# A decoder trunk in fp32r products: twelve norms summed by two fp32r products with ones, and the engines' order planned anew with a table of moved groups

## The chip, the cores and the metric

The kernel runs on one core of one Trainium2 chip. The metric is the device time of one execution in microseconds (us), the median over runs. The core has five engines with an instruction stream each: TensorE (PE; its weight loads are PEld in the profile), VectorE (DVE), ScalarE (ACT), GpSimd (POOL) and SyncE (SP, which here only issues DMAs). They wait for each other through semaphores, and each of them takes its instructions strictly in the order in which they stand in its stream.

## The reference

Two layers of a decoder trunk over one sequence of 1024 tokens with 1024 channels, in float32:

```
for l in range(DEPTH):
    h = rmsnorm(x, attn_norm[l]);  proj = h @ w_in[l]
    y_a = mla_attention(...)        # 4 heads, latent q and kv with norms of their own, rope, causal
    y_b = short_gated_conv(...)     # width 3
    y_c = multiscale_pool(...)      # trailing means over 2, 4, 8, 16
    y_d = swa_sink_attention(...)   # window 128, ALiBi, sinks
    mixed = rmsnorm of each of the four groups (256 channels each) * mix_norm
    x = x + mixed @ w_o[l]
    h2 = rmsnorm(x, ffn_norm[l]);  gate, up = split(h2 @ w_gate_up[l])
    x = x + (silu(gate) * up) @ w_down[l]
return rmsnorm(x, final_norm)
```

rmsnorm(x) is x / sqrt(mean(x*x) + 1e-6) times a gain, over the channels. d_ff is 2816.

## The kernel before

All activations lie with channels on the 128 partitions and tokens along the free dimension; a token half is 512 columns, and a tile of 128 x 512 float32 fills one of the eight PSUM banks. A product of two float32 operands is made of three fp32r products (`mm3`, line 270): each operand is split into a high part (a copy to fp32r on ACT, line 281 or, with a gain, 284) and a low part (the difference, on DVE, line 282 or 285); high*high, high*low and low*high are summed in PSUM. `half_split` does that for one tile of 128 x 512, into two half slots of a pool of 47 pairs of SBUF slots. Weights are loaded by SP and split in the same way (`weights`, lines 213 and 214, and others). The FFN's products are made by a Strassen-like scheme with fewer block products; POOL makes the sums of weights and some of the elementwise products.

A norm needs the sum of squares over all channels. `SumSq.add` (lines 311 to 322) squares a tile on ACT and adds it on DVE to an accumulator of 128 x 512, and `rnorm` sums the accumulator over the partitions with one float32 matmul with a 128 x 128 matrix of ones (line 328), which leaves the sum on all partitions of a bank. In the trace such a float32 matmul stands in two rows. Then ACT takes Ln, Exp and Square (lines 330 to 332) and DVE finishes with a Newton step (333 and 336). The factor is multiplied in after the projection, so the products that follow a norm don't wait for it, only the evacuations of their banks do. There are 35 norms: two at the entry (`enter_norm`), in each layer twelve of groups, latent q and kv and the attention output (`group_scale`, `sq_kv`, `sq_q`, `norm_a`), two of the FFN's input (`norm`), two between the layers, and three at the end, where the last token half goes in two pieces of 256 columns.

The program is written once in a plain order. `order_engines` (line 1914) then decides in what order each engine issues: `steps_of` turns the instructions into steps (neighbouring float32 matmuls onto the same bank are one step) with their dependences and an estimated length, and `arrange` is a list scheduler that plays the five engines against each other in time. A step enters when its inputs are ready and its tiles have a buffer; of the ready steps of an engine that with the lowest rank, its place in the program, is issued. Its prices are tables: 226.7 ns for a product 512 wide, 867 ns for a float32 one with ones, 92 ns for changing over to float32 steps, hand-overs of 25 to 80 ns between engines, DMA landings by size, and others. The result is fixed by extra dependences from each instruction to the one before it on its engine. Buffers of a tag (the PSUM banks: 2 `mm`, 3 `s`, 2 `t`, 1 `pv`) are handed out in the order of the program whatever the ranks are.

In time: 0 to 25 us the entry, to about 400 the first layer's attention part (the projections and short mixers, then from about 200 on the MLA heads with scores at lines 888 to 890, transposes at 942, values at 954 and the pieces of the output projection), to about 1050 its FFN, to about 1420 the second layer's attention part, to 2050 its FFN, and then the last norm and stores.

Of the kernel before, what the change touches and what calls it, by code (L numbers as in the profile page):

```python
# [18 lines left out]
P = 128  # L19
# [92 lines left out]
def trunk_kernel(ctx: ExitStack, tc: tile.TileContext, ins, out):  # L112
# [20 lines left out]
    ident = cst[:, CC_ID : CC_ID + P]  # L133
    ones = cpool.tile([P, P], F32, name="ones")
    dve.memset(ones, 1.0)
    e_r = cpool.tile([P, P], F32R, name="e_r")
    nsink = cpool.tile([P, L * 4], F32, name="nsink")
    nffn = cpool.tile([P, L * NK], F32, name="nffn")
# [157 lines left out]
    class SumSq:  # L296
# [24 lines left out]
            else:  # L321
                dve.tensor_tensor(out=a, in0=a, in1=q, op=ALU.add)

        def rnorm(self, t, cols=whole, tag="t"):

            a, n = F.ap(self.acc[t])[:, cols], self.n
            p = ps(tag)[:, cols]
            pe.matmul(p, ones, a, start=True, stop=True)  # L328
            r0, q = tmp("tn")[:, cols], tmp("tn")[:, cols]
            act.activation(r0, p, AF.Ln, scale=1.0 / n)  # L330
# [30 lines left out]
    def enter_norm(t):  # L361
        for k in range(NK):
            ss.add(t, F.ap(xf[k][t]))
            F.free(xf[k][t])
        ratt[t] = ss.rnorm(t)

    def finish(x, t, cols):

# [10 lines left out]
    for l in range(L):  # L379
# [644 lines left out]
        def norm_a(t):  # L1024
            for c in range(2):
                sg.add(t, F.ap(y["a"][c][t]))
            r = sg.rnorm(t)
            ma = []
            for c in range(2):
                a = F.ap(y["a"][c][t])  # L1030
                mul_to(a, a, F.ap(r))
                ma.append(half_split(a, pcol(l, PC_MIX + c)))
                F.free(y["a"][c][t])
            F.free(r)
            return ma
# [377 lines left out]
                    cur.extend(dn_acts_split(*r))  # L1413

        def norm(u):
            r2.append(F.ap(ss2.rnorm(HALVES[u], tag="pv")))

        std.append(GateUp(2))
        plain(0, 0)
# [162 lines left out]
        for n, (c, m) in enumerate(units):  # L1582
            if n < 5:
                for _ in range(3):
                    next(sums, None)
            if n + 2 < len(units):
                raws.append(dn_raw(*units[n + 2]))
            if c in fresh:
                u, t = fresh[c]
                d = 2 * m + u  # L1590
                x[d][t] = F.half()
                sp.dma_start(F.ap(x[d][t]), xr[d][:, t * HT : (t + 1) * HT])
            if n + 1 < len(units):
# [12 lines left out]
            for j in range(NG):  # L1606
                accumulate(p, w, c, j)
                if m == NM - 1:
                    for s in cur[j]:
                        R.free(s)  # L1610
            for v in w:
                v.free()
            evac(c, m, p)
            for _ in range(2):
                if cn is not None and m < NM - 1:
                    nxt.extend(dn_acts(cn, (len(nxt) + 1) // 2))
            if m == NM - 1:
                cur, nxt = nxt, []
            if c == T3:
                done(2 * m, 0)  # L1620
            elif c == T4:
                done(2 * m + 1, 0)
                done(2 * m + 1, 1)
            elif c == B22:
                done(2 * m, 1)
                if m == 0:
                    expect_layer(l + 1)
                    ahead()
                if m == 1:
                    ratt[0] = ss.rnorm(0, tag="pv")  # L1630
                if m == NM - 1:
                    ratt[1] = ss.rnorm(1, tag="pv")
# [20 lines left out]
    "SP": {"PE": 50, "DVE": 35, "ACT": 35, "POOL": 80, "SP": 30},  # L1653
}
OVERLAP = {"DVE": 82, "ACT": 97, "POOL": 44}
FUNC_SETS = {"Silu": "Silu", "Exp": "Exp", "Ln": "Exp"}
ENGINES = {"PE": "PE", "DVE": "DVE", "Activation": "ACT", "Pool": "POOL", "SP": "SP"}


class Step:  # L1660
    __slots__ = ("ins", "eng", "rank", "before", "after", "tiles", "left", "ns", "tail", "ready", "sums", "bank", "onchip", "size", "start", "end", "table", "ls", "slotafter")

    def __init__(self, eng, rank):
        self.ins, self.eng, self.rank = [], eng, rank
        self.before, self.after, self.tiles = set(), [], set()
# [3 lines left out]
        self.table = None  # L1669


def areas(a):
# [60 lines left out]
def steps_of(tc):  # L1733
    steps, seen = [], {}
    table, runs = None, {"Silu": [], "Exp": []}
    for i in tc.nc.cur_bb.bb.instructions:
# [14 lines left out]
        if eng == "PE":  # L1751
            n = width(outs[0])
            if fp32:
                one = i.ins[1].bass_ap.tensor.name.startswith("ones")
                v.ns += (867 if n == 512 else 534) if one else 108
                v.tail = 163 if one else 122
            else:
                v.ns = MM_NS[n]
                v.tail = 164 if n > 128 else 173
        elif kind == "InstDMACopy":  # L1760
            v.size = 4
            for s, n in outs[0].ap:
                v.size *= int(n)
            if eng == "POOL":
                v.ns, v.tail = 700, 4200
        else:
            v.ns = length(eng, kind, i, ins, outs)
            v.onchip = not any(a.bass_ap.tensor.name.startswith("ps_") for a in ins + outs)
            if eng == "ACT" and len(outs) > 1:
                v.tail = 61  # L1770
        f = FUNC_SETS.get(str(getattr(i, "func", "")).split(".")[-1])
# [8 lines left out]
        for a, writes in [(a, False) for a in ins] + [(a, True) for a in outs]:  # L1780
# [5 lines left out]
            if name.split("_")[0] not in DRAM_TILES:  # L1786
                v.tiles.add(name)
            seen.setdefault(name, [])
            for r, w, u in seen[name]:
                cross = name.startswith("ps_") and not (w or writes)  # L1790
                if cross or (w or writes) and any(
                    x[0] < y[1] and y[0] < x[1] and x[2] < y[3] and y[2] < x[3]
                    for x in r
                    for y in rects
                ):
                    v.before.add(u)
            seen[name].append((rects, writes, v))
    for v in steps:
        v.before.discard(v)
    return steps  # L1800


def arrange(steps, rank=lambda v: v.rank):
# [20 lines left out]
    now = {e: [] for e in SIGNAL}  # L1824
    out = {e: [] for e in SIGNAL}
    wire, pool_busy, last_fp32, table = 0.0, [], False, "Exp"
    for v in steps:
        if not v.left:
            heapq.heappush(later[v.eng], (0.0, rank(v), v.rank, v))
    while any(now.values()) or any(later.values()):  # L1830
        best = None
        for e in SIGNAL:
# [9 lines left out]
        while later[e] and later[e][0][0] <= t:  # L1842
            _, k, n, v = heapq.heappop(later[e])
            heapq.heappush(now[e], (k, n, v))
        k, n, v = heapq.heappop(now[e])
        wait = None
        for name in v.tiles - live:
# [11 lines left out]
        for name in v.tiles - live:  # L1859
            tag = name.rsplit("_", 1)[0]  # L1860
            live.add(name)
            queue[tag].popleft()
# [5 lines left out]
        if v.size:  # L1868
            if e == "SP":
                free[e] = t + 450  # L1870
                wire = max(t + 1400, wire) + v.size / 330.0
                v.end = wire + 600
            else:
                free[e] = t + v.ns
                v.end = t + v.ns + v.tail
# [4 lines left out]
            v.end = s + v.ns + v.tail  # L1880
        else:
            ns = v.ns
            if e == "DVE" and v.onchip:
                ns += 0.8 * sum(max(0.0, min(b, t + ns) - max(a, t)) for a, b in pool_busy[-8:])
            if v.table and v.table != table:
# [6 lines left out]
            if v.tail:  # L1892
                free[e] = v.end - 10
                v.end += v.tail
        out[e].append(v)
        for name in v.tiles:
            todo[name] -= 1
            if not todo[name]:
                tag = name.rsplit("_", 1)[0]
                heapq.heappush(freed[tag], max(u.end for u in uses[name]))  # L1900
                for x in parked[tag]:
                    heapq.heappush(later[x[2].eng], (t + 1, *x))
# [8 lines left out]
    assert sum(map(len, out.values())) == len(steps)  # L1911
    return out

def order_engines(tc):

    info = mybir.DependencyInfo(mybir.DependencyClass.NoSync, mybir.DependencyReason.DATA)
    for queue in arrange(steps_of(tc)).values():
        last = None
        for v in queue:
            for i in v.ins:  # L1920
# [131 lines left out]
```

## Time and profile before

| | |
|---|---|
| median of 3 runs | 2083.02 us (2080.73 to 2083.82) |
| profiled execution | 2081.12 us, span 2079.3 us |
| granted TensorE clock | 0.998 of full |
| PE, DVE, ACT, POOL busy | 2051.7, 1529.5, 968.0, 571.9 us |
| matmuls | 9442 |
| moved by DMA | 289.76 MB, 139 GB/s |

A row of the profile's timeline has the start, the time and the engine, then the line, operation, tile written and tiles read, shapes and how many neighbouring instructions of that kind are merged; in brackets stands the idle time of the engine before it and who ended it. A row of groups has the busy time, the mean duration of one in ns, and the idle time before them. A row of stages (windows) has, for each engine, its busy us and its number of instructions. Matmuls are pipelined: their rows overlap, and a busy PE can still be short of its peak.

### The profile page before, as it was taken

How to read it: one execution, taken by the hardware profiler on the slowest of the kernel's cores; microseconds unless marked ns; L12 is line 12 of the kernel's file. 1: busy time of each engine (PE TensorE's matmuls, PEld its weight loads, DVE VectorE, ACT ScalarE, POOL GpSimd, SP SyncE). 2: the span in 40 equal slices, each digit the busy share in tenths (PEclk: the TensorE clock that was granted, in tenths of full speed). 3: DMA queues.
4: the chain of work that ended last, by engine and by line, in shares of the span. 5: the costliest groups of instructions: out<-in, count | busy, mean ns of one | idle time of the engine just before them, and what ended most of it. 6: DMA issues, size and time to landing. Idle time of an engine off the chain costs nothing.

```text
span 2079.3 us, 26320 instructions
## 1 busy us (share of the span) xinstructions
PE 2051.7 (99%) x9442; PEld 1679.6 (81%) x9442; DVE 1529.5 (74%) x2407; ACT 968.0 (47%) x1700; POOL 571.9 (28%) x453
## 2 busy tenths in 40 slices
PE   8999999999999999999999999999999999999997
PEld 6887777888888888888888877778888888888887
DVE  7878977977776777655657898869777677686555
ACT  6447656643333334444433566656433333354342
POOL 0000000037776775100000000000567677650000
PEclk9999999999999999999999999999999999999999
DMA  4110222424444446966401102232354444398652
GB/s 180 34 51 26 76 83 71 162 80 171 174 155 144 167 162 228 339 233 206 148 27 53 46 16 91 68 118 101 123 185 149 151 167 157 133 323 311 198 177 89
DMA packets 148819, 289.76 MB, mean 139 GB/s; under 512 B 12608, under 2 KB 72000, under 8 KB 148688
## 3 DMA queue, kind: packets, MB, share of 16 engines
q1 hardware_dynamic: 148656, 288.03, 40.1%
q8 instruction: 74, 1.21, 0.2%
q14 instruction: 57, 0.47, 0.1%
q0 software_dynamic: 32, 0.04, 0.0%
HBM read 204.66 MB, written 83.36 MB: 139 GB/s over the span
## 4 chain that ended last, share of the span: by engine, by line
PE 92%; DVE 6%; ACT 1%; DMA 1%; issue 0%; DVEq 0%; ACTq 0%; SPq 0%
PE ps_mm L270 34%; PE ps_s L270 29%; PE ps_t L270 12%; PE ps_pv L270 8%; PE ps_pv L954 2%; PE ps_t L942 1%; DVE u L282 1%; PE ps_s L888 1%; PE ps_pv L564 1%; PE ps_t L328 1%; PE ps_mm L762 1%; PE ps_s L503 1%; PE ps_s L890 1%; PE ps_s L889 1%; DVE u L340 1%; PE ps_t L552 1%
## 5 line engine op out<-in xcount | busy, mean ns | idle before, releaser
L270 PE MATMUL ps_mm<-u,u 128*128 128x512 f32 (+1 forms) x3376 | 825.8, 391 | 9.3 <-ACT u L284 7.1
L270 PEld LDWEIGHTS ps_mm<-u,u 128*128 128x128 f32 x3376 | 617.0, 189 | 131.6 <-ACT u L284 7.1
L270 PE MATMUL ps_s<-u,u 128*128 128x512 f32 x2672 | 630.7, 390 | 0.0
L270 PEld LDWEIGHTS ps_s<-u,u 128*128 128x128 f32 x2672 | 501.6, 188 | 106.3 <-issue 2.2
L282 DVE TENSOR_TENSOR u<-u,u 128x1024 fp32r<-128x1024 f32 (+2 forms) x368 | 443.4, 1230 | 148.7 <-ACT u L281 124.5
L281 ACT CAST u<-u 128x1024 fp32r<-128x1024 f32 (+2 forms) x368 | 321.1, 897 | 476.1 <-PE ps_mm L270 195.8
L270 PE MATMUL ps_t<-u,u 128*128 128x512 f32 (+1 forms) x1212 | 274.4, 379 | 0.0
L270 PEld LDWEIGHTS ps_t<-u,u 128*128 128x128 f32 x1212 | 219.1, 188 | 43.5 <-issue 1.4
L951 POOL MEMSET u<- 128x128 f32 x32 | 6.1, 217 | 865.8 <-PE ps_mm L270 628.8
L159 POOL TENSOR_TENSOR u<-u 128x256 f32<-128x256 f32 x176 | 188.4, 1071 | 68.9 <-DMA u<-in_w_dn 39.8
L1304 POOL TENSOR_TENSOR tp<-tp,u 128x512 f32<-128x512 f32 x88 | 144.0, 1638 | 223.2 <-ACT tp L1303 223.0
L270 PE MATMUL ps_pv<-u,u 128*128 128x512 f32 x696 | 164.9, 389 | 0.0
L270 PEld LDWEIGHTS ps_pv<-u,u 128*128 128x128 f32 x696 | 130.7, 188 | 27.1
L1303 ACT ACTIVATE tp<-tp 128x512 f32<-128x512 f32 x88 | 55.4, 632 | 119.6 <-DVE tp L340 118.6
L1124 POOL TENSOR_TENSOR u<-u,u 128x512 f32<-128x512 f32 x38 | 66.1, 1739 | 144.0 <-DMA u<-in_w_gu 81.9
L284 ACT ACTIVATE u<-u,par 128x512 fp32r<-128x512 f32 x100 | 69.9, 717 | 51.5 <-DVE u L1091 16.9
L282 DVE TENSOR_TENSOR u<-ps_t,u 128x512 fp32r<-128x512 f32 (+4 forms) x136 | 77.5, 584 | 21.7 <-ACT u L281 20.9
L281 ACT CAST u<-ps_t 128x512 fp32r<-128x512 f32 (+4 forms) x136 | 66.7, 505 | 57.0 <-PE ps_t L942 36.0
L285 DVE SCALAR_TENSOR_TENSOR u<-u,par,u 128x512 fp32r<-128x512 f32 x100 | 73.2, 751 | 8.3 <-ACT u L284 8.1
L1516 DVE TENSOR_TENSOR tp<-ps_mm,tn 128x512 f32<-128x512 f32 x38 | 26.3, 692 | 68.7 <-PE ps_mm L270 68.7
L214 DVE TENSOR_TENSOR u<-u,u 128x1024 fp32r<-128x1024 f32 (+1 forms) x46 | 51.8, 1129 | 33.2 <-ACT u L213 12.9
L1146 POOL TENSOR_TENSOR u<-u 128x512 f32<-128x512 f32 x38 | 68.3, 1797 | 8.9 <-DVE u L282 8.9
(186 smaller groups left out, 2240.2 us busy)
## 6 DMA issues: line engine op xcount, KB each, us to landing
u<-in_w_gu SPq DMA_DIRECT2D x88, 512.0 KB, 4.3
ad<-u SPq DMA_DIRECT2D x154, 256.0 KB, 2.5
u<-ad SPq DMA_DIRECT2D x70, 512.0 KB, 5.2
u<-in_w_dn SPq DMA_DIRECT2D x68, 512.0 KB, 3.9
qd<-u SPq DMA_DIRECT2D x44, 512.0 KB, 2.9
u<-qd SPq DMA_DIRECT2D x32, 512.0 KB, 4.7
u<-in_w_in SPq DMA_DIRECT2D x30, 512.0 KB, 3.5
u<-in_xT SPq DMA_DIRECT2D x32, 256.0 KB, 4.8
```

The lines of the kernel that those rows point to most:

```text
L159: pool.tensor_tensor(out=o, in0=o, in1=u, op=ALU.add)
L214: dve.tensor_tensor(out=lo[:, :n], in0=raw[:, :n], in1=rd(hi[:, :n]), op=ALU.subtract)
L270: pe.matmul(o, w, r, start=start and k == 0 and i == 0, stop=stop and k == n - 1 and i == 2, skip_group_check=again,)
L281: act.copy(hi, f)
L282: dve.tensor_tensor(out=lo, in0=f, in1=rd(hi), op=ALU.subtract)
L284: act.activation(hi, f, AF.Copy, scale=gain)
L285: dve.scalar_tensor_tensor(out=lo, in0=f, scalar=gain, in1=rd(hi), op0=ALU.mult, op1=ALU.subtract)
L954: pe.matmul(py[:, c0:], v_of(j, h), R.ap(s)[:, c0:], start=j == 0 and n == 0, stop=j == nj - 1 and n == 1,)
L1124: pool.tensor_tensor(out=F.ap(q + 1), in0=a21, in1=a22, op=ALU.add)
L1146: pool.tensor_tensor(out=q4, in0=q4, in1=F.ap(self.raw[1] + 1), op=ALU.add)
L1303: last_silu = act.activation(g, g, AF.Silu)
L1304: pool.tensor_tensor(out=g, in0=g, in1=r, op=ALU.mult)
```

## The change

Three things change.

The sum over partitions. `rnorm` gets a flag `parts`. With it, the accumulator is split into a high and a low fp32r half (ACT copy, DVE difference), and two fp32r products with ones rounded to fp32r sum both into the bank in place of the float32 matmul. The flag is set at the entry, for the attention output (`norm_a`), for the FFN's input and between the layers: 2 + 4 + 4 + 2 = 12 of the 35.

The planner's prices and rules. On ACT and DVE an instruction that starts on other partitions than the one before it (`rows`) starts a gap later (`SHIFT`); DMAs of up to 128 KB land 1700 ns, not 600, after the wire; two writes of the same bank are ordered like two reads of it; dependences that another one covers are dropped; a float32 step that is ready is taken next after a float32 step; tiles are held in a list and not a set.

The table. `places` numbers groups of steps (one engine, one bank or tile, not over 60 places apart) and gives 408 of them a place some ranks earlier (321) or later (87); the list scheduler sorts by place.

```diff
+    ones_r = cpool.tile([P, P], F32R, name="ones_r")
+    dve.tensor_copy(ones_r, ones)
...
-        def rnorm(self, t, cols=whole, tag="t"):
+        def rnorm(self, t, cols=whole, tag="t", parts=False):
...
-            pe.matmul(p, ones, a, start=True, stop=True)
+            if parts:
+                h, lo = half_split(a)
+                for k, i in enumerate((h, lo)):
+                    pe.matmul(p, ones_r, R.ap(i), start=k == 0, stop=k == 1)
+                    R.free(i)
+            else:
+                pe.matmul(p, ones, a, start=True, stop=True)
...
+SHIFT = {"DVE": 31, "ACT": 24, "POOL": 0}
...
+            if ins:
+                v.rows = tuple(areas(a)[1][0][0] for a in (ins[0], outs[0]))
...
-                cross = name.startswith("ps_") and not (w or writes)
+                cross = name.startswith("ps_") and w == writes
...
+        if e == "PE" and last_fp32 and not v.sums:
+            alike = [x for x in now[e] if x[2].sums and takes(x[2], t)]
+            if alike:
+                heapq.heappush(now[e], (k, n, v))
+                now[e].remove(min(alike))
+                k, n, v = min(alike)
+                heapq.heapify(now[e])
...
-                v.end = wire + 600
+                v.end = wire + (1700 if v.size <= 131072 else 600)
...
+            if v.rows:
+                rows, end = before[e]
+                if rows != v.rows and (rows[1] or v.rows[0]):
+                    t = max(t, end + SHIFT[e])
...
+MOVES = {
+    3: -96, 6: -115, 11: -89, 16: -86, 27: -169, 31: -105, 36: -107, 51: -110, 56: 17, 65: -242,
...
+    4613: -139,
+}
+
+
+def places(steps):
+
+    groups, last, at = {}, {}, {}
+    for v in steps:
+        k = v.bank, v.eng
+        if k not in groups or v.rank - last[k] > 60:
+            groups[k] = len(at)
+            at[groups[k]] = None
+        last[k] = v.rank
+        v.place = v.rank + MOVES.get(groups[k], 0)
+    return steps
...
-    for queue in arrange(steps_of(tc)).values():
+    for queue in arrange(places(steps_of(tc)), lambda v: v.place).values():
```

More of the change, by code (lines that the diff above doesn't have):

```diff
@@ L364, in enter_norm @@
             F.free(xf[k][t])
-        ratt[t] = ss.rnorm(t)
+        ratt[t] = ss.rnorm(t, parts=True)
     def finish(x, t, cols):
@@ L1026, in norm_a @@
                 sg.add(t, F.ap(y["a"][c][t]))
-            r = sg.rnorm(t)
+            r = sg.rnorm(t, parts=True)
             ma = []
@@ L1415, in norm @@
         def norm(u):
-            r2.append(F.ap(ss2.rnorm(HALVES[u], tag="pv")))
+            r2.append(F.ap(ss2.rnorm(HALVES[u], tag="pv", parts=True)))
         std.append(GateUp(2))
@@ L1629, in trunk_kernel @@
                 if m == 1:
-                    ratt[0] = ss.rnorm(0, tag="pv")
+                    ratt[0] = ss.rnorm(0, tag="pv", parts=True)
                 if m == NM - 1:
-                    ratt[1] = ss.rnorm(1, tag="pv")
+                    ratt[1] = ss.rnorm(1, tag="pv", parts=True)
         for cols in (slice(0, 256), slice(256, HT)) if last else ():
@@ L1660 @@
 class Step:
-    __slots__ = ("ins", "eng", "rank", "before", "after", "tiles", "left", "ns", "tail", "ready", "sums", "bank", "onchip", "size", "start", "end", "table", "ls", "slotafter")
+    __slots__ = ("ins", "eng", "rank", "before", "after", "tiles", "left", "ns", "tail", "ready", "sums", "bank", "onchip", "size", "start", "end", "table", "rows", "place")
     def __init__(self, eng, rank):
         self.ins, self.eng, self.rank = [], eng, rank
-        self.before, self.after, self.tiles = set(), [], set()
+        self.before, self.after, self.tiles = set(), [], []
         self.ns = self.tail = self.ready = self.size = 0
@@ L1668, in __init__ @@
         self.onchip = False
-        self.table = None
+        self.table = self.rows = None
 def areas(a):
@@ L1785, in steps_of @@
                 continue
-            if name.split("_")[0] not in DRAM_TILES:
-                v.tiles.add(name)
+            if name.split("_")[0] not in DRAM_TILES and name not in v.tiles:
+                v.tiles.append(name)
             seen.setdefault(name, [])
             for r, w, u in seen[name]:
-                cross = name.startswith("ps_") and not (w or writes)
+                cross = name.startswith("ps_") and w == writes
                 if cross or (w or writes) and any(
@@ L1799, in steps_of @@
         v.before.discard(v)
+    spare = [{u for w in v.before for u in w.before if u in v.before} for v in steps]
+    for v, far in zip(steps, spare):
+        v.before -= far
     return steps
@@ L1826, in arrange @@
     wire, pool_busy, last_fp32, table = 0.0, [], False, "Exp"
+    before = {e: ((0, 0), 0.0) for e in SHIFT}
     for v in steps:
@@ L1829, in arrange, with takes @@
             heapq.heappush(later[v.eng], (0.0, rank(v), v.rank, v))
+    def takes(v, t):
+        for name in (x for x in v.tiles if x not in live):
+            tag = name.rsplit("_", 1)[0]
+            if queue[tag][0] != name or not freed[tag] or freed[tag][0] + 40 > t:
+                return False
+        return True
     while any(now.values()) or any(later.values()):
@@ L1845, in arrange @@
         k, n, v = heapq.heappop(now[e])
+        if e == "PE" and last_fp32 and not v.sums:
[5 more added lines that the diff above has]
+                heapq.heapify(now[e])
         wait = None
-        for name in v.tiles - live:
+        for name in (x for x in v.tiles if x not in live):
             tag = name.rsplit("_", 1)[0]
@@ L1858, in arrange @@
             continue
-        for name in v.tiles - live:
+        for name in [x for x in v.tiles if x not in live]:
             tag = name.rsplit("_", 1)[0]
@@ L1894, in arrange @@
                 v.end += v.tail
+            if v.rows:
+                before[e] = v.rows, v.end
         out[e].append(v)
@@ L1901, in arrange @@
                 for x in parked[tag]:
-                    heapq.heappush(later[x[2].eng], (t + 1, *x))
+                    heapq.heappush(later[x[2].eng], (v.start + 1, *x))
                 parked[tag] = []
```

46 rows, old and new, of the table MOVES are left out of this document.

## The prediction

> **What bounds the kernel now.** I read the totals of the page first, then the busy time by stage, then, in the stages where TensorE has gaps, its instructions in order of time.
>
> ```profile
> span 2079.3 us, 26320 instructions
> PE 2051.7 (99%) x9442; PEld 1679.6 (81%) x9442; DVE 1529.5 (74%) x2407; ACT 968.0 (47%) x1700; POOL 571.9 (28%) x453
> ```
>
> ```profile
> core 0: us, PE busy (x) PEld busy (x) DVE busy (x) ACT busy (x) POOL busy (x), PEclk, DMA share, GB/s
> 0.00:25.00 25.00, 17.83 (x69) 14.19 (x70) 19.11 (x33) 20.69 (x32) 0.91 (x5) 1.00 0.88 320
> 25.00:200.00 175.00, 173.34 (x826) 138.01 (x825) 139.58 (x322) 95.18 (x215) 0.00 (x0) 1.00 0.12 41
> 200.00:350.00 150.00, 146.31 (x724) 116.14 (x723) 131.47 (x320) 94.46 (x222) 2.61 (x14) 1.00 0.23 75
> 350.00:400.00 50.00, 50.00 (x228) 39.75 (x228) 38.81 (x61) 28.34 (x47) 0.41 (x2) 1.00 0.41 147
> 400.00:1050.00 650.00, 650.00 (x2864) 537.21 (x2863) 454.70 (x494) 269.86 (x371) 284.51 (x208) 1.00 0.52 181
> 1050.00:1230.00 180.00, 179.59 (x861) 144.88 (x860) 130.79 (x308) 88.15 (x203) 0.00 (x0) 1.00 0.11 35
> 1230.00:1375.00 145.00, 141.10 (x696) 112.33 (x697) 126.33 (x310) 89.53 (x212) 2.71 (x14) 0.99 0.24 75
> 1375.00:1420.00 45.00, 45.00 (x208) 35.99 (x207) 31.82 (x51) 24.28 (x41) 0.41 (x2) 1.00 0.40 141
> 1420.00:2050.00 630.00, 630.00 (x2831) 523.16 (x2830) 444.05 (x484) 252.54 (x351) 280.40 (x208) 1.00 0.51 179
> 2050.00:2080.00 30.00, 18.57 (x150) 17.91 (x148) 12.81 (x32) 4.94 (x12) 0.00 (x0) 0.88 0.25 86
> ```
>
> TensorE sets the end. In the FFN stages (400 to 1050, 1420 to 2050) it takes 2864 matmuls in 650.00 us, 0.227 us each: no order can win anything there. What an order can win lies in the attention stages, 25 to 400 and 1050 to 1420. The idle that the rows show there is 1.66 + 3.69 + 0.41 + 3.90 = 9.7 us. It is too small a number, because a wide matmul's row is 0.39 us long while the next starts 0.227 us after it, so that each shown wait hides another 0.16 us and shorter ones don't show. So I counted by shape. The stretch from 200 to 350 has 22 groups of matmuls; first and last of them:
>
> ```profile
> L270 PE MATMUL ps_mm<-u,u 128*128 128x512 f32 x296 | 78.9, 401 | 0.3 <-ACT u L213 0.2
> ```
>
> ```profile
> L954 PE MATMUL ps_pv<-u 128*128 128x512 f32 x2 | 0.9, 446 | 0.6 <-ACT u L281 0.6
> ```
>
> ```profile
> 2059.79 8.08 PE L270 MATMUL ps_mm<-u,u 128*128 128x256 f32 x66
> ```
>
> ```profile
> 1364.29 0.60 PE L942 MATMUL ps_t<-cst,u 128*128 128x128 f32 x4
> 1364.64 0.48 PE L888 MATMUL ps_s<-u,u 128*128 128x512 f32 x1
> 1364.96 0.40 PE L889 MATMUL ps_s<-u,u 128*128 128x512 f32 x1
> ...
> 1365.42 0.60 PE L942 MATMUL ps_t<-cst,u 128*128 128x128 f32 x4
> 1366.58 0.50 PE L954 MATMUL ps_pv<-u 128*128 128x512 f32 x1 [0.56 <-ACT u L281]
> 1367.58 0.63 PE L942 MATMUL ps_t<-cst,u 128*128 128x128 f32 x4 [0.50 <-DVE u L282]
> 1367.97 0.47 PE L954 MATMUL ps_pv<-u,u 128*128 128x512 f32 x1
> 1369.34 0.80 PE L270 MATMUL ps_mm<-u,u 128*128 128x512 f32 x2 [0.89 <-ACT u L213]
> ```
>
> The groups hold 460 matmuls 512 wide at 0.227, 96 of 256 at 0.120 (66 of them in 8.08 us, the last 0.28 long), 36 of 384 at an estimated 0.173, 124 transposes at 0.109 (four end 0.60 after they start, the last 0.27 long) and four norms at 0.87 (below): 104.4 + 11.5 + 6.2 + 13.5 + 3.5 = 139.1. TensorE lost 10.9 of 150 us. The same count gives, from 25 on and stage by stage, 6.7, 11 to 11.6, 0.7, then in the second layer 4.4, 12.9 and 0.9: together 37 us in the attention stages, nothing in the FFN.
>
> The last rows show what such a loss is. The transposes of 1365.42 are through at 1365.86; the product of 1366.58 waits for the split of their result, 0.72 us; after it the next four transposes wait again. Then a product waits for a weight split, and behind that stands a load:
>
> ```profile
> 1362.81 5.57 DMA u<-in_w_o
> ```
>
> ```profile
> PE ps_mm L270 <- DVE u L821: 2.4, 2, 1.2
> ```
>
> The second row, of the waits, says that twice (once a layer) a product waits 1.2 us for DVE's evacuation of the values. All of these are waits behind an in-order engine that another order could fill.
>
> **The change, part A: twelve norms.** The norms with the new path are two at the entry (the first at 31.28), two of the attention output, two before the FFN in each layer, and two between the layers: 2 + 4 + 4 + 2 = 12 of 35.
>
> ```profile
> L328 PE MATMUL ps_t<-u,ones x52: 590/592/697, 31.3 to 1399.8; 128*128 128x512 f32 x52
> L328 PE MATMUL ps_pv<-u,ones x14: 590/592/611, 397.9 to 2039.1; 128*128 128x512 f32 x14
> ```
>
> ```profile
> 31.28 1.02 PE L328 MATMUL ps_t<-u,ones 128*128 128x512 f32 x2
> 31.74 3.53 PE L270 MATMUL ps_s<-u,u 128*128 128x512 f32 x13
> ```
>
> ```profile
> L779 PE MATMUL ps_t<-u,e_r x8: 389/392/497, 186.9 to 1219.6; 128*128 128x512 f32 x8
> ```
>
> One fp32 norm stands in two rows. The 13 products after it end at 35.27, so the last starts at 34.88 and, 12 steps of 0.227 earlier, the first could have started its stream at 32.15: the norm took 32.15 - 31.28 = 0.87 us. Two fp32r products take 2 x 0.227 = 0.454 us; the form is there already, e_r at line 779, 0.392 long like any other. Removed: 12 x (0.87 - 0.454) = 5.0 us, all of it on TensorE, hence on the path. The number of matmul rows stays 9442. The Trainium skill (TensorE: Matmul & The Clock Gate, Back-to-back issue gap) gives about 131 ns for one 512-wide matmul in a sustained stream of loads and matmuls; by that estimate part A would be 12 x (0.87 - 0.262) = 7.3 us. This trace does not agree, with 227 ns over 2864 in a row.
>
> Added: twelve splits of 128 x 512.
>
> ```profile
> L281 ACT CAST u<-u 128x512 fp32r<-128x512 f32 x60 | 37.2, 621 | 205.3 <-PE ps_mm L270 165.6 <-DVE u L710 26.8 <-POOL u L1125 4.7
> L282 DVE TENSOR_TENSOR u<-te,u x20: 677/685/693, 179.0 to 1349.5; 128x512 fp32r<-128x512 f32 x20
> ```
>
> ACT gets 12 x 0.62 = 7.5 us and DVE 12 x 0.69 = 8.2 us; both have room (968.0 and 1529.5 of 2079.3). One copy of ones costs well under a microsecond on DVE at the start, where loads set the pace (DMA share 0.88). The sum of a norm now comes later: by 0.62 + 0.69 and a hand-over or two of some 0.05, less the 0.64 that the matmul itself gains, since only the second product (0.23, not 0.87) comes after the split: about 0.75 us. On ACT and DVE the work behind the split moves by as much at worst. What covers it is TensorE's own queue:
>
> ```profile
> 1399.34 1.10 PE L328 MATMUL ps_t<-u,ones 128*128 128x512 f32 x2
> ...
> 1399.88 4.44 PE L270 MATMUL ps_mm<-u,u 128*128 128x512 f32 x17
> 1400.48 0.60 ACT L330 ACTIVATE tn<-ps_t 128x512 f32<-128x512 f32 x1 [2.00 <-PE ps_t L328]
> ```
>
> Here 17 and more products of another group run on while ACT and DVE work on the norm, and the six norms before the FFN and between the layers (on bank pv, the first at 397.9) lie in or beside gapless stages. Bounds: nothing, and 12 x 0.75 = 9.0 if every norm were awaited. I take 0.5 us, near nothing, since only the two entry norms and the attention ones lie where waits are common. Two more R halves are held for some 2 us each; nothing near them waits for a slot.
>
> **Part B: the order.** The planner now charges a gap for a change of partitions on ACT and DVE (24 and 31 ns), lands DMAs of up to 128 KB 1.1 us later, ties writes to one PSUM bank to each other, and takes a ready fp32 step next behind an fp32 step. Then 408 groups get another place, 321 of them earlier, none of them from 1362 to 2354, in the numbering of the groups. No instruction comes or goes by this: it is worth exactly what it takes from, or adds to, the 37 us.
>
> Taking fp32 steps together I cost at nothing. From the four transposes of 1364.29 to the product of 1364.96 is 0.67 us, and 4 x 0.109 + 0.227 is 0.66: changing over costs 0.01.
>
> Named waits: 2.7 for the two behind line 821 (2.4 shown and 0.16 each), 1.1 behind the load (0.89 shown; from 1368.20 to 1369.34 by starts), and the two of the chain at 1366 and 1367, 0.72 + 0.77 by starts, which the first layer has as well (rows below): 3.0, together 6.8 us. The rest, 30 us, is hundreds of waits of 50 to 400 ns, of which some 5 must stay: TensorE lost 0 to 1.5% even where nothing was short. I take half of the named and a quarter of the 25 others: 3.4 + 6.2 = 9.6 us. The ends are a gain of 32 (all but the floor) and a loss of 12 (below). The value is a choice: the waits in the rows are short ones between engines, 0.05 to 1.2 us, and a plan that is off by a few tens of ns per hand-over can remove the long ones but not most short ones.
>
> ```profile
> 341.17 0.50 PE L954 MATMUL ps_pv<-u 128*128 128x512 f32 x1 [0.61 <-ACT u L281]
> 342.14 0.63 PE L942 MATMUL ps_t<-cst,u 128*128 128x128 f32 x4 [0.47 <-DVE u L282]
> ```
>
> The ends (7 us before the first matmul, 9 after the last) are loads, and the last norm and its stores; I cost them at nothing.
>
> **Sum.** -5.0 + 0.5 - 9.6 = -14.1 us. The profiled execution took 2081.1 us (span 2079.3), 1.9 below the median of 2083.0. So 2067.0 for it and 2068.9 for the median.
>
> **Rivals.** *The order gives nothing on the chip.* Every wait removed comes back elsewhere, because bank turns and ACT and DVE set it and not the order; for this speak the gapless ACT and DVE between 200 and 350 (131.5 and 94.5 us of 150 is no slack for chains), against it the load of 5.57 us on the path, which an earlier issue cures. Time: 2083.0 - 4.5 = 2078.5.
>
> *The order is worse.* TensorE is in order, so one step planned too early holds all behind it. With 408 groups moved for a planned time, the stretches from 200 to 350 and 1230 to 1375 could lose half as much again: 24 / 2 = 12 us. It decides from 4.5 us on, where it has eaten part A; time 2083.0 - 4.5 + 12 = 2090.5. For it speaks that 25 to 400 and 1050 to 1420 lose alike today (19 and 18 us) under one planner, so its errors are systematic; against it that the two layers differ in single waits only.
>
> *The order gives most of it*, 22 of the 32: 2083.0 - 4.5 - 22 = 2056.5. Against it: the short waits.
>
> **How the numbers follow.** Runs spread by 3 us, so 0.2% (4.2 us, below 2078.9) is about what can be told from no change. Forecast 0.60, with its own range 2061 to 2076 (half to one and a half times part B, rounded); order without effect 0.18, half of it on either side of the 0.2%; order worse 0.13, of which 0.03 stays within 0.2%; most of it 0.09. Faster 0.60 + 0.09 + 0.09 = 0.78, same 0.09 + 0.03 = 0.12, slower 0.10. The range reaches from 2056 to 2081: it leaves out the worse order and some of the cases beyond 22 us, some 0.18.
>
> **What would show it.** Line 328's fp32 rows fall from 70 to 46 and 24 fp32r rows with ones_r stand in their place, 0.39 long; matmuls stay 9442; ACT gains 12 instructions and DVE 13. By the same count the attention stages lose some 28 us and not 37, with the 1.2 us wait behind line 821 and the wait behind w_o gone first; the FFN stages stay gapless. I am wrong if waits of PE behind Ln, Exp or the norm's last products appear (part A), or if the losses by stage are as large as before at other places (part B).

## The result and the profile after

The changed kernel takes 2063.5 us (2062.8 to 2064.5), the kernel before, on the same chip, 2082.5: a ratio of 0.991, 95% interval 0.9893 to 0.9927, some 19 us. Forecast were 14, in a range of 2056 to 2081. The profiled execution took 2062.8 us.

The head of the page:

```profile
span 2061.0 us, 26301 instructions
PE 2038.0 (99%) x9442; PEld 1680.9 (82%) x9442; DVE 1539.8 (75%) x2420; ACT 971.0 (47%) x1712; POOL 571.3 (28%) x453
```

The groups of the norms, a row for each form:

```profile
L336 PE MATMUL ps_t<-u,ones x40: 590/592/682, 163.4 to 1249.8; 128*128 128x512 f32 x40
...
L333 PE MATMUL ps_t<-u,ones_r x12: 389/392/477, 24.6 to 1382.5; 128*128 128x512 f32 x12
L333 PE MATMUL ps_pv<-u,ones_r x12: 389/392/412, 413.0 to 1442.2; 128*128 128x512 f32 x12
```

The number of matmuls is the same, and 24 of them are fp32r products with ones_r, as long as any other. Of the float32 rows 46 are left: these 40, two on the bank pv and four of 256 columns at the end. ACT has 12 instructions more and DVE 13. The busy time by stage:

```profile
core 0: us, PE busy (x) PEld busy (x) DVE busy (x) ACT busy (x) POOL busy (x), PEclk, DMA share, GB/s
...
200.00:330.00 130.00, 129.81 (x660) 106.16 (x659) 115.29 (x283) 82.12 (x198) 2.36 (x12) 1.00 0.22 71
330.00:425.00 95.00, 94.82 (x440) 78.31 (x440) 76.87 (x129) 56.07 (x97) 0.69 (x4) 1.00 0.34 122
425.00:500.00 75.00, 72.71 (x317) 58.50 (x316) 59.71 (x61) 30.42 (x44) 50.05 (x36) 1.00 0.44 153
...
1225.00:1375.00 150.00, 149.66 (x770) 123.50 (x770) 130.92 (x317) 93.73 (x222) 2.88 (x16) 1.00 0.25 79
...
1425.00:2030.00 605.00, 605.00 (x2718) 502.58 (x2717) 423.72 (x449) 237.20 (x326) 280.93 (x208) 1.00 0.52 181
```

In the MLA stages the rows of TensorE now show hardly a gap: 0.19 us of idle in 130 and 0.34 in 150, where the kernel before showed 3.7 in 150 and 3.9 in 145. And where it had none, from 425 to 500, there are 2.3 us. By the count of the prediction (the stretch less each matmul at its cadence, from all starts), the time that TensorE lost is, in us:

| | attention 1 (25 to 425) | FFN 1 (425 to 525) | attention 2 (1050 or 1025 to 1425) |
|---|---|---|---|
| before | 19.1 | 0 | 18.2 |
| changed | 9.6 | 3.9 | 9.8 |

So 37.3 became 19.4 in the attention stages, 17.9 won; 3.9 went in the FFN; the cheaper sums are 5.0. 17.9 - 3.9 + 5.0 = 19.0; the spans differ by 18.3, the rest lies at the two ends.

Some 1.7 of the 17.9 were no wait. In the profiled execution of the kernel before, the granted clock of TensorE was 0.50 from 1369.87 to 1373.29 us, right behind the waits at 1366.58, 1367.58 and 1369.34 that the prediction shows, and matmuls came at about half their pace. The changed kernel's execution has no such stretch until its matmuls are through.

What was won can be sorted by length. A wait is here the time from when a matmul's predecessors were through, at their cadences, to its own start; the stretch at half clock is left out. (Cadences here: 0.2267, 0.174, 0.120 us for 512, 384 and 256 columns, 0.108 for a transpose, 0.868 for a float32 sum, so that the sums with the half clock are 36.0 and 18.5 us.)

| waits in the two attention stages | before | changed |
|---|---|---|
| under 0.05 us | 7.9 us | 8.3 us |
| 0.05 to 0.4 us | 147, 16.2 us | 82, 8.0 us |
| over 0.4 us | 13, 10.2 us | 3, 2.2 us |

Who TensorE waits for (us in all, times, the longest):

```profile
PE ps_s L272 <- ACT u L286: 7.4, 1, 7.4
PE ps_s L336 <- DVE u L320: 1.4, 1, 1.4
PE ps_mm L272 <- DVE u L1001: 1.2, 1, 1.2
PE ps_s L272 <- DVE te L1512: 1.0, 1, 1.0
PE ps_s L272 <- DVE tp L348: 0.5, 1, 0.5
...
PE ps_mm L272 <- DVE u L829: 0.2, 1, 0.2
PE ps_mm L272 <- ACT u L215: 0.2, 1, 0.2
```

The first row is the first load, as before, the second the last norm. The wait behind the evacuation of the values (L821 before, L829 now) went from 2.4 to 0.2 us, that behind the split of the weights (L213, now L215) from 1.1 to 0.2. One of 1.2 us is new, behind an evacuation in the output projection (L1001, at 1395.03). The chain of transposes and splits at the end of the first attention, which stood still twice for more than half a microsecond, now looks like this:

```profile
332.49 0.60 PE L950 MATMUL ps_t<-cst,u 128*128 128x128 f32 x4
332.84 0.71 PE L962 MATMUL ps_pv<-u,u 128*128 128x512 f32 x2
333.39 0.40 PE L897 MATMUL ps_s<-u,u 128*128 128x256 f32 x2
333.62 0.46 PE L962 MATMUL ps_pv<-u 128*128 128x512 f32 x1
333.92 0.40 PE L962 MATMUL ps_pv<-u,u 128*128 128x512 f32 x1
334.16 0.40 PE L898 MATMUL ps_s<-u,u 128*128 128x256 f32 x2
334.39 0.93 PE L950 MATMUL ps_t<-cst,u 128*128 128x128 f32 x7
335.50 0.73 PE L272 MATMUL ps_mm<-u,u 128*128 128x512 f32 x2 [0.18 <-ACT u L215]
```

Scores of another block (L897, L898) stand between a transpose and the product that needs its split.

### The profile page after: what moved, and what is told of

It reads as the page before. It is cut to its first block, busy times and chain, and to the rows that moved or that the text cites. A ratio compares the mean times of both kernels' runs of the same rounds, so it can differ in the third digit from the quotient of the medians.

```text
span 2061.0 us, 26301 instructions
## 1 busy us (share of the span) xinstructions
PE 2038.0 (99%) x9442; PEld 1680.9 (82%) x9442; DVE 1539.8 (75%) x2420; ACT 971.0 (47%) x1712; POOL 571.3 (28%) x453
## 4 chain that ended last, share of the span: by engine, by line
PE 95%; DVE 2%; ACT 1%; DMA 1%; issue 1%; POOL 0%; DVEq 0%; SPq 0%; ACTq 0%; POOLq 0%
PE ps_mm L272 36%; PE ps_s L272 29%; PE ps_t L272 12%; PE ps_pv L272 8%; PE ps_pv L962 2%; PE ps_t L950 1%; PE ps_s L896 1%; PE ps_t L336 1%; PE ps_s L897 1%; PE ps_s L898 1%; PE ps_pv L572 1%; PE ps_mm L770 1%; PE ps_s L511 1%; DVE u L284 1%; PE ps_t L560 1%
## 5 line engine op out<-in xcount | busy, mean ns | idle before, releaser
L272 PE MATMUL ps_mm<-u,u 128*128 128x512 f32 (+1 forms) x3376 | 835.5, 389 | 1.4 <-DVE u L1001 1.2
L284 DVE TENSOR_TENSOR u<-u,u 128x1024 fp32r<-128x1024 f32 (+2 forms) x380 | 449.5, 1206 | 154.1 <-ACT u L283 118.9
L283 ACT CAST u<-u 128x1024 fp32r<-128x1024 f32 (+2 forms) x380 | 328.1, 888 | 480.4 <-PE ps_mm L272 192.8
L272 PE MATMUL ps_t<-u,u 128*128 128x512 f32 (+1 forms) x1212 | 284.1, 378 | 0.0
L284 DVE TENSOR_TENSOR u<-ps_t,u 128x512 fp32r<-128x512 f32 (+4 forms) x136 | 76.9, 582 | 18.4 <-ACT u L283 17.6
L348 DVE TENSOR_TENSOR tp<-tp,u 128x512 f32<-128x512 f32 x76 | 69.0, 908 | 1.1
L318 ACT ACTIVATE tn<-u 128x512 f32<-128x512 f32 (+1 forms) x93 | 52.8, 589 | 31.8 <-DVE u L1577 28.4
```

The source lines that it names most:

```text
L272: pe.matmul(o, w, r, start=start and k == 0 and i == 0, stop=stop and k == n - 1 and i == 2, skip_group_check=again,)
L283: act.copy(hi, f)
L284: dve.tensor_tensor(out=lo, in0=f, in1=rd(hi), op=ALU.subtract)
L318: act.activation(q, f, AF.Square)
L348: dve.tensor_tensor(out=o, in0=a, in1=b, op=ALU.mult)
```

## The experiments

All times are medians; the kernel before stood at 2081.5 to 2082.0 us beside them. Where two kernels of different calls are compared, the difference is that of the medians, and can be off by about a microsecond. The first four take the change apart.

**The norms alone.** The kernel before with the new path for the twelve norms.

```diff
-            pe.matmul(p, ones, a, start=True, stop=True)
+            if parts:
+                h, lo = half_split(a)
+                for k, i in enumerate((h, lo)):
+                    pe.matmul(p, ones_r, R.ap(i), start=k == 0, stop=k == 1)
```

> The kernel before with the twelve norms on the new path, ordered by the planner of before. The prediction's theory (the products take 5.0 us off TensorE, the later sums cost 0.5): about 2078.5, a ratio of 0.998. Rival 1 (the later sums are awaited, up to 9 us): 2082 or more. Rival 2 (the five us that the prediction missed come from the norms too, because the planner has more to fill gaps with): 2073 or less.

Measured: 2080.3, ratio 0.9996 (0.9987 to 1.0005): no difference that can be told, and the expected 0.998 lies outside. The five us came off the matmuls, but TensorE lost 44.4 us between its first and its last matmul, not 40.7. A row of its waits, which the kernel before has not:

```profile
PE ps_mm L272 <- DVE u L348: 2.3, 1, 2.3
```

and its place in the timeline, at the second entry norm:

```profile
44.36 0.69 DVE L320 SCALAR_TENSOR_TENSOR u<-tn,u 128x512 f32<-128x512 f32 x1
44.97 0.68 DVE L348 TENSOR_TENSOR u<-ps_mm,u 128x512 f32<-128x512 f32 x1
45.08 0.62 ACT L283 CAST u<-u 128x512 fp32r<-128x512 f32 x1 [2.22 <-DVE u L320]
45.71 0.50 PE L272 MATMUL ps_mm<-u,u 128*128 128x512 f32 x1 [2.28 <-DVE u L348]
...
46.98 6.78 PE L272 MATMUL ps_t<-u,u 128*128 128x512 f32 x22
```

The product waits for a bank of mm, and its evacuation (L348) stands on DVE behind the last add of the second norm (L320): with the later sums the planner has put it there. The wait is three times the 0.75 us by which a sum was estimated to be late. It also stands in the kernels without moves in the first layer (e2 and e7 below), and not in the changed kernel.

More stands behind it. The 22 products of the last row took 6.78 us, where 21 steps of 0.227 and a row of 0.39 are 5.16: in this execution the granted clock (PEclk, the first of the last three numbers) was 0.50 from 47.17 to 50.58 us:

```profile
47.17:50.58 3.41, 3.41 (x9) 2.65 (x9) 1.35 (x2) 1.86 (x3) 0.00 (x0) 0.50 0.01 2
```

The wait with its hidden 0.16 and the 1.6 us of half clock are 4.0, where the kernel before lost 1.6 in all from 25 to 50 us. The rest of the 3.7 that were lost more was not traced.

**The table away.** The changed kernel with MOVES empty.

```diff
+MOVES = {}
```

> The changed kernel with an empty table: the norms, and the new prices and rules of the planner. The prediction's theory (the rules alone are worth nothing, the table carries the order's gain): the time of e1 within 2 us, about 2078. Rival (the new prices for partition changes and small loads carry it): 2070 or less.

Measured: 2076.2, ratio 0.9976 (0.9965 to 0.9987). Neither: 4 us under the norms alone, so the rules are worth something, and 12.7 above the changed kernel, so the table carries most. TensorE lost 19.8 and 18.4 us in the two attention stages, much as before the change. Of the 18.4, some 3.4 are two stretches of 3.41 us at half clock, from 1253.27 and from 1365.91 us.

**The moves in the first FFN away.**

```diff
+MOVES = {k: v for k, v in MOVES.items() if not 1200 <= k <= 1361}
```

> The changed kernel without the moves of groups 1200 to 1361, which lie in the first part of the first layer's FFN. There the changed kernel loses some 3.6 us on TensorE (425 to 500 us) that the kernel before did not lose, and the second layer's FFN, whose groups have no moves, loses nothing. Theory (these moves make the loss): about 2060, with no loss from 425 to 500. Rival (the later r of the FFN's norms makes it): 2063.5 as before, the loss stays.

Measured: 2060.1 (2059.3 to 2061.7), ratio 0.9896 (0.9881 to 0.9910), as expected. The stage from 425 to 500 is gapless, while its norms are still on the new path:

```profile
425.00:500.00 75.00, 75.00 (x333) 62.10 (x332) 61.99 (x64) 30.64 (x43) 54.74 (x38) 1.00 0.44 152
```

These moves cost the changed kernel 3.4 us by the medians, 2.9 by the ratios. This version is faster than both kernels. It also shows how far the count of a single execution can be off: attention 2 lost 1.9 us more here than in the changed kernel, with the same order on TensorE.

**The float32 sum in the new order.** The splits stay, their results are not used.

```diff
-                for k, i in enumerate((h, lo)):
-                    pe.matmul(p, ones_r, R.ap(i), start=k == 0, stop=k == 1)
-                    R.free(i)
+                pe.matmul(p, ones, a, start=True, stop=True)
+                for i in (h, lo):
+                    R.free(i)
```

> The changed kernel with the splits of the twelve norms left in (their results unused) and one float32 matmul with ones in place of the two products; table and rules as changed. The prediction's theory (a float32 sum costs 0.41 us more of TensorE each, all of it on the path): 2063.5 + 5.0 = 2068.5. Rival (part of it falls into waits that are there anyway, and the sum no longer waits for the split): 2066 or less.

Measured: 2067.6, ratio 0.9933 (0.9916 to 0.9949), 4.1 above the changed kernel. Near the theory: in an order that fills the waits, nearly all of the 5.0 us is paid on the path. With the old order it was 1.3.

The next two ask where the norms' gain went under the old planner.

**Six norms alone** (before the FFN and between the layers; the diff is against the norms alone).

```diff
-        ratt[t] = ss.rnorm(t, parts=True)
+        ratt[t] = ss.rnorm(t)
...
-            r = sg.rnorm(t, parts=True)
+            r = sg.rnorm(t)
```

> The kernel before, its planner, and only the six norms before the FFN and between the layers on the new path. Theory (the norms alone won only 1 us because the later sums are awaited at the entry and at the attention output, not here): 6 x 0.41 = 2.5 us, about 2079 against 2081.5, ratio 0.9988. Rival (the later sum costs about the same at every norm): half of e1's gain, 2081.

Measured: 2079.1 (2077.7 to 2085.3), ratio 0.9993 (0.9983 to 1.0002). The median is where the theory has it and TensorE lost 40.6 us, as before, but the runs spread by 8 us and the interval holds no change as well. The three runs over 2081 us had a granted clock of 0.996 or 0.997, the seven others, 2077.7 to 2079.2, of 0.998 or 0.999.

**Two entry norms alone.**

```diff
-        ratt[t] = ss.rnorm(t)
+        ratt[t] = ss.rnorm(t, parts=True)
```

> The kernel before, its planner, and only the two entry norms on the new path. Theory (the later factor lets a product wait for a bank of mm, 2.3 us in e1's trace): 0.8 won, some 2.9 lost from 0 to 50 us, about 2083.5, ratio 1.001. Rival (that wait belongs to the order of the whole and not to these norms): 2080.7.

Measured: 2082.5, ratio 1.0002 (0.9992 to 1.0011). The time can't tell. The trace can: the wait of 2.3 us behind L348 is there with these two norms alone, and not with the six.

**The table for the second layer alone.**

```diff
+MOVES = {k: v for k, v in MOVES.items() if k > 1361}
```

> The changed kernel with the table only for groups over 1361, which are the second layer and the end. Theory (what a move wins lies at its own stage): the first layer loses on TensorE what e2 lost (some 11 from 200 to 350), the second what the changed kernel lost (some 5): 2076.2 - 8.6 = 2067.6. Rival (the table works as a whole, a plan of the first layer decides the second's): 2072 or more.

Measured: 2070.9, ratio 0.9948 (0.9933 to 0.9963), between the two. The stages, without the table and with half of it:

```profile
200.00:350.00 150.00, 145.30 (x729) 116.69 (x728) 132.43 (x322) 95.47 (x225) 2.71 (x14) 1.00 0.24 75
1225.00:1375.00 150.00, 145.55 (x718) 116.94 (x717) 129.27 (x315) 92.92 (x218) 3.08 (x14) 0.98 0.23 72
```

```profile
200.00:350.00 150.00, 145.89 (x728) 117.06 (x727) 133.73 (x324) 96.95 (x227) 2.73 (x14) 1.00 0.23 75
1225.00:1375.00 150.00, 148.91 (x757) 121.84 (x756) 132.75 (x321) 94.02 (x223) 2.86 (x16) 1.00 0.24 75
```

The first layer has 4.1 us of shown idle of its 4.7 without the table, the second 1.1 of 4.4: a stage wins by its own moves. By the count attention 2 lost 11.4 and not 18.4. That is 7.0 of the 8.6 expected, but the two stretches at half clock in e2's execution are 3.4 of it (the 0.98 in the second row of the first view); the medians differ by 5.3.

Then, why the moves in the first FFN lose. In the changed kernel's timeline there:

```profile
469.19 2.28 POOL L1132 TENSOR_TENSOR u<-u,u 128x512 f32<-128x512 f32 x1
470.25 1.77 DVE L348 TENSOR_TENSOR tp<-tp,u 128x512 f32<-128x512 f32 x1
471.94 0.68 DVE L1512 TENSOR_TENSOR te<-ps_s,tn 128x512 f32<-128x512 f32 x1
...
472.68 5.74 PE L272 MATMUL ps_s<-u,u 128*128 128x512 f32 x24 [0.99 <-DVE te L1512]
```

A DVE product that takes 0.68 us elsewhere takes 1.77, the evacuation behind it comes that much later, and TensorE, whose products were moved ahead, waits for the bank.

**POOL at its price in the rows.**

```diff
-        return 206 if kind == "InstMemset" else 230 + 2.07 * n
+        return 206 if kind == "InstMemset" else 424 + 2.53 * n
```

> The changed kernel with its whole table and one price changed: a POOL instruction costs 424 + 2.53 n ns and not 230 + 2.07 n, which is 1.07 us at 256 and 1.72 at 512, as the rows of the trace have it (1.07; 1.36 to 1.76). Theory (the moves in the first FFN lose 3.5 us because the plan thinks that POOL is done 0.4 us earlier than it is, and puts products behind banks that POOL's results free): 2060, no loss from 425 to 500. Rival (the moves lose there whatever POOL is thought to cost): 2063.5.

Measured: 2064.2, ratio 0.9916 (0.9902 to 0.9931); from 425 to 525 TensorE still lost 3.0 us. The theory fell: that POOL is thought too fast is not the cause. With the right price TensorE's order came out the same in all but 6 of its 9442 places, so POOL's real length was not tried here.

**POOL that writes and does not read.**

```diff
-            pool.tensor_tensor(out=g, in0=g, in1=r, op=ALU.mult)
+            pool.memset(g, 0.01)
...
-                pool.tensor_tensor(out=o, in0=o, in1=u, op=ALU.add)
+                pool.memset(o, 0.01)
```

> The changed kernel with its table, and each sum and product of POOL replaced by a fill of the same output with a constant (the outputs are not the reference's): POOL writes the same tiles, but reads none. Theory (in 425 to 500 us of the changed kernel a DVE instruction with two inputs in SBUF stands still while POOL reads, 1.77 us for 0.68, and the moved products wait behind it): the loss there falls from 3.9 to under 1, and such DVE rows are 0.7 long. Rival (the moves lose there by their order alone): 3 us or more remain. The whole may gain more than these 3 us, since nothing waits for POOL.

The planner keeps POOL's old prices for these fills, so that the order stays.

Measured: 2059.9 (two runs), and 0.5 us lost from 425 to 525 in place of 3.9, with TensorE's order the same in all but 4 places. DVE's rows, of the changed kernel and then of this one, min/median/max in ns:

```profile
L348 DVE TENSOR_TENSOR tp<-tp,u x76: 677/738/1775, 470.2 to 1837.5; 128x512 f32<-128x512 f32 x76
...
L348 DVE TENSOR_TENSOR tp<-ps_s,u x6: 676/678/684, 441.3 to 1471.0; 128x512 f32<-128x512 f32 x6
```

```profile
L348 DVE TENSOR_TENSOR tp<-tp,u x76: 681/689/695, 467.5 to 1833.0; 128x512 f32<-128x512 f32 x76
```

With two inputs in SBUF the product takes up to 1.78 us while POOL adds; with one of them in PSUM 0.68 at most, in three of the six while POOL adds or multiplies; and once POOL reads nothing, 0.70 at most in all 76. So DVE stands still behind POOL's reads, as the theory has it. The Trainium skill (SBUF — State Buffer, Who interferes with whom) states that a VectorE instruction with two SBUF inputs contends with a GpSimd instruction that reads SBUF, not with one that only writes it; these rows agree in both halves. POOL itself is also quicker here (0.53 us for a fill 512 wide, 1.36 to 1.76 for a sum), so how much of the 3.4 us is DVE's standstill and how much POOL's length isn't told apart.

The standstill alone loses nothing. The kernel before has it too:

```profile
L340 DVE TENSOR_TENSOR tp<-tp,u x76: 677/693/1761, 472.7 to 1856.0; 128x512 f32<-128x512 f32 x76
```

Its FFN stages are gapless all the same, and so is the stage in e3, where such rows take up to 1.22 us from 425 to 525. What loses is the standstill in an order that puts products behind it: e3 takes the one away, e9 the other, and the loss goes with either.

**The rules alone.**

```diff
+MOVES = {}
...
-        ratt[t] = ss.rnorm(t, parts=True)
+        ratt[t] = ss.rnorm(t, parts=False)
```

(and so at the other norms)

> The changed kernel with an empty table and all norms by the float32 matmul: the planner's new prices and rules alone. Prediction's theory (worth nothing): 2081.5. Rival (e2's gain over e1 is theirs): 2078.

Measured: 2078.5 (2074.7 to 2082.8), ratio 0.9983 (0.9973 to 0.9993): the rival. The new prices and rules win some 3.5 us without table and norms. In the profiled execution attention 2 lost 14.0 us in place of 18.2, but 1.7 of these 4.2 are the half clock that the execution of before has there; this one has 3.41 us of it in attention 1, from 230.75 us. Without these stretches both stages won some 2.5 us.

**The table under the old prices.**

```diff
-SHIFT = {"DVE": 31, "ACT": 24, "POOL": 0}
+SHIFT = {"DVE": 0, "ACT": 0, "POOL": 0}
...
-                v.end = wire + (1700 if v.size <= 131072 else 600)
+                v.end = wire + 600
```

> The changed kernel with its table, but no gap for a change of partitions and 600 ns, as before, for the landing of small DMAs. Theory (the table is a list of exceptions to one plan: a place in a list that is sorted by readiness means something only with the prices that it was searched with): much of the gain goes, 2068 to 2074, with waits back from 325 to 400 us. Rival (a move is a priority and holds under any price): within 2 us of 2063.5.

Measured: 2072.9, ratio 0.9957 (0.9940 to 0.9974), 9.4 above the changed kernel, as the theory has it: attention 1 lost 18.4 us, 4.8 of them from 350 to 425.

**The lock in the planner, and a table searched anew.**

```diff
+            if e == "DVE" and v.two:
+                t = max([t] + [b for a, b in pool_busy[-4:] if a <= t < b])
+                dve_busy.append((t, t + ns))
+            if e == "POOL" and v.two:
+                t = max([t] + [b for a, b in dve_busy[-4:] if a <= t < b])
```

> The changed kernel with one more rule in its planner (a DVE instruction and a POOL instruction with two inputs in SBUF each exclude one another in time, in place of a stretch of 0.8 of the overlap) and a table searched anew in the planner under that rule, with no moves in the FFN from 425 us on. Theory (the loss at 425 to 500 was the planner's blind spot, and all else was already close to what the order can give): no loss from 425 to 500 and the time of e3, 2060 within 1.5. Rival (the pricing of POOL also held back the rest): 2057 or less.

Measured: 2063.9, ratio 0.9915 (0.9898 to 0.9931). No loss from 425 to 525, as expected, but 1.8 and 1.4 us more than e3 in attention 1 and 2: neither e3's time nor less. The new table has 1504 moves and none in this stretch, so the missing loss there is no more than e3 had shown; and since rule and table changed together, it can't be said which of the two made the rest worse (by an amount, stage for stage, no larger than that by which single executions differ; the medians differ by 3.8). The best version stays e3.

## Why the prediction was right, and where it was off

*The bound.* Right: what was won lies in the stages that were named, and TensorE's FFN rows had nothing to give. The 37 us held 1.7 at half clock, which the prediction took for waits. "No order can win anything there" left out that an order can lose there: 3.9 us, 3.4 by e3. None of the rivals had it, and it is a term of its own that the table brought.

*Part A, the matmuls.* Right: 24 rows of 0.392, the count unchanged, 4.1 us measured in the new order (e4) for 5.0 less 0.5. Of the two costs of a matmul 512 wide that were weighed, the trace's 0.227 is what fits: from the start of one of the 24 rows to the next matmul's it is 0.231 us in the median.

*Part A, the cover.* "I take 0.5 us, near nothing" held only for the order of the changed kernel. In the order of before, TensorE lost 3.7 us more with the later sums, a good part of it one wait and the half clock behind it, and the norms alone win nothing that can be told (e1). The rows shown for the cover were those of an attention norm with 17 products behind it; at the entry, where the planner now queued a bank's evacuation behind the second norm's adds, there was none, and the step did not look at who evacuates its banks.

*Part B, grouping and rules.* "No instruction comes or goes by this" is so; but the working priced only the fp32 grouping, at nothing, and put all gain on the table. The rules alone win 3.5 us (e10). Which of them isn't settled.

*Part B, the sum.* This is the term that was mis-sized. Order, forecast 9.6; measured 13.9 (e4 against before), or 17.3 without the moves that lose. Nearly all of the named waits went, some 6 of their 6.8 us and not half, and of the 30 others some 10 and not 6, beside the 1.7 of half clock. The reason given was that a plan off by tens of ns can't remove most short waits. The table of waits by length speaks against it: those of 0.05 to 0.4 us fell by half, from 16.2 to 8.0 us. They were 147 and not the hundreds that the prediction spread its 30 us over. What the order did not touch are the steps under 0.05 us, 8 us and not the 5 of the prediction's floor.

*The total.* It came within 5 us partly by luck: the order won 7.7 us more than forecast where it wins, and the FFN, at which nothing was forecast, lost 3.4. The forecast's own range, 2061 to 2076, is said to be half to one and a half times part B; by the sum that would be 2064 to 2074, and 2061 to 2076 is about half to one and a half times the whole 14.1.

*The rivals.* "The order gives nothing" fell with e2 against the changed kernel (12.7 us); its row did not bear it out either, since ACT with 94.5 us of 150 is far from gapless. "The order gives most of it", 22 us, was not reached. "The order is worse" did happen, in one stretch of 100 us, in the way that was named (a step planned too early holds all behind it), at a stage that was thought closed.

## What to carry to other kernels

When one in-order engine is 99% busy, count its loss from starts and cadence and not from idle shown: that showed 37 us where the rows showed 10, and nearly half of it could be had by order alone. Look at the granted clock before calling a loss a wait. A cheaper instruction with a later result is worth its price only where something fills the new wait; measure it in the order that it will run in (1.3 us in one, 4.1 in the other). A table of exceptions belongs to the prices that it was searched with (9.4 us lost under others), and moves in a stage without loss are better left out: they cost 3.4 us here.

## What was not expected of the hardware

A DVE product of 128 x 512 with both inputs in SBUF took up to 1.78 us beside POOL's sums, 0.68 with one input in PSUM, and 0.70 at most once POOL only wrote (e9).

Behind a cluster of waits the clock can be at half. Six executions of kernels without the whole table (before, e1, e2, e6, e7, e10) have between them seven stretches of 3.41 us at a granted clock of 0.50 in mid-program, some 1.7 us each. In the 5 us before each of them TensorE waited for 1.8 us or more in all. Not every such wait has one behind it: e1, e6 and e7 have one behind the 2.4 us at the entry, e2 has the same wait at 45.54 us and none there. None of the executions with the whole table, or all of it but the moves in the FFN (the changed kernel, e3, e4, e8, e9), has one, and neither have e5, e11 and e12.

The spread of runs goes with the same clock. The kernels without the table spread by 2.7 to 8.0 us (e1, e2, e5, e6, e10; 7 to 10 runs each), those with a whole one by 0.7 to 2.7 (the changed kernel, e3, e4, e8, e11, e12; 4 runs each, which may make some of that). In e1 the runs with a granted clock of 0.998 took 2079.5 to 2080.0 us, those with 0.996 2081.9 to 2082.2; in e10 the one at 0.998 took 2074.7, the one at 0.995 2082.8. That the waits start such a stretch fits all of this but was not tried.
